# A two-layer hybrid attention block on one Trainium2 core: pooling sums and late forget gates on VectorE, and a planner without its margin

## Chip, core and metric

The kernel runs on one core of a Trainium2 chip, as one program. The metric is the device time of one execution in microseconds; the time of a kernel is the median of several runs.

## What is computed

1024 tokens of width 1024 behind 16 meta tokens (1040 rows) go through two layers. A layer normalizes, projects to 3588 columns, and splits them into three mixers: forgetting attention (4 heads of 64, with a decay `c` summed from forget gates), differential attention (4 heads with two softmaxes each, causal by chunks), and pooling over sliding windows of 2, 4, 8 and 16 rows. Gated outputs go through an output projection and are added to the residual. The reference pads to 1152 rows and cuts again, which the kernel need not do. Cut to what matters here:

```python
for l in range(DEPTH):
    hn = rmsnorm(h, norm_g[l])
    proj = jnp.einsum('bld,de->ble', hn, w_in[l])
    fq, fk, fv, fz, fg, dq, dk, dv, dz, pu, pz = jnp.split(proj, IN_OFFSETS, axis=-1)
    log_f = jax.nn.log_sigmoid(fg.astype(jnp.float32) + b_f[l].astype(jnp.float32))
    c = jnp.transpose(jnp.cumsum(log_f, axis=1), (0, 2, 1))
    a_out = forgetting_attention(...fq, fk, fv, c) * jax.nn.silu(fz)
    b_out = differential_attention(...dq, dk, dv, lam)
    b_out = (rmsnorm(b_out, subln_g[l], SUBLN_EPS) * (1.0 - lambda_init)) * jax.nn.silu(dz)
    c_out = pooling_mixer(pu, w_pool[l], pool_scale[l]) * jax.nn.silu(pz)
    mix = jnp.concatenate([a_out, b_out, c_out], axis=-1)
    h = h + jnp.einsum('ble,ed->bld', mix, w_out[l])
y = rmsnorm(h[:, N_META:N_META + S], final_g)

def pooling_mixer(u, w_pool, pool_scale):
    ...
    pooled = (cs - lower) / cnt[None, :, :, None] - uf
    y = jnp.einsum('blgc,gcd->blgd', pooled.astype(u.dtype), w_pool)
    return y.reshape(B, Lp, POOL_W) * pool_scale
```

## The kernel before

**Precision and projections.** Every float32 product is made of three matmuls of split operands: a rounded high part and the low rest of each side (high x high, high x low, low x high). ScalarE copies the high part, VectorE or GpSimd subtracts to get the low one. The normalized input is held transposed in SBUF as `HT` (high and low part, 8 blocks of 128). A projection item (`proj_chunk`) has 128 output columns in three chunks of some 346 rows; a chunk is 24 matmuls of `HT` and a weight tile `ws` into a PSUM bank `psP`, of which there are two, and an evacuation. So a matmul group can start only when the bank two groups ahead has been read.

**Units.** A layer has six attention units of 128 columns: two of forgetting attention, four of differential. While the projections of a unit run, the attention of the unit before it is slipped in between their matmuls, in steps: scores into `psS` (three banks), softmax on VectorE and ScalarE into `p`, transposes of `p` into `psT` (two banks), a copy and a subtraction into `pp`, and products with the values into `psO` (one bank). A unit of forgetting attention has eight tasks, one of differential attention four: 64 tasks in two layers. The meta tokens' share of a task goes its own way: `thrice` copies 32 columns of `p` three times into `m3`, TensorE transposes 96 columns, and `ptm` gets two high parts and a low one (`meta_t`, `meta_av`).

**Pooling.** Beside the last unit run four more items (`pool_item`, `pool_gate`). `pool_item` writes two halves `Y[1]`, then `Y[0]`; `pooling` makes the window sums of one half by shifted adds between rows `wa` and `wb` (four for `Y[1]`, two for `Y[0]`; on GpSimd), with a copy on ScalarE, and a scaled sum on VectorE back into `Y`. `pool_mix` splits `Y` into `pu` (ScalarE, then VectorE), multiplies with `w_pool` in `mix` (three matmuls in a `psP` bank) and evacuates on VectorE, scaled by `sc`. `pool_gate` then multiplies `Y` by the silu of its gate.

**Output projection.** `out_proj` keeps `w_out` in the place of `HT` and makes eight tiles of 128 rows and one of 16 for the meta rows, 48 matmuls of 512 columns for a full one. VectorE adds the residual into `res`, `rms` normalizes it in place, and beside the last tile of layer 0 `to_hnT` starts to transpose the normalized rows into `HT` for layer 1 (bank `psS`, ScalarE copies, VectorE subtracts).

**Forget gates.** `forget_gates` gives 36 columns to TensorE: three chunks of 16 matmuls with `wg` at the head of a layer, then a copy, an add, and `gate_sums`, which writes the running sums `c` to DRAM, from where the first two units load them as `cb`.

**Order.** Two planners in the kernel set it. `Planner.run` writes the program: after every six matmuls of a projection it takes the attention steps whose inputs a coarse clock (`Clock`) holds ready, with `MARGIN` nanoseconds added. `Order` then lists all instructions with costs of its own and sets each engine's order anew: TensorE's instructions lie in a few lines, each with a fixed order (projections, three queues of steps, deferred ones, transposes for `HT`), and the head that can go first is taken; among heads that can all go at once the one written first. The DMA queue of SyncE is ordered in the same way. Engines run strictly in that order.

```python
heads = [(self.when(q[0]) + MARGIN, q) for q in self.queues if q]
due = [q for t, q in heads if t <= clk.now and (q[0]["target"] <= spent or not live)]
```

## Time and profile before

| what | value |
|---|---|
| median of 3 runs | 1239.56 us (1238.59 to 1240.54) |
| profiled execution | 1240.62 us |
| its span | 1238.8 us |
| TensorE busy | 1199.4 us, 97% (7644 matmuls) |
| VectorE busy | 805.1 us, 65% |
| ScalarE busy | 628.4 us, 51% |
| GpSimd busy | 499.1 us, 40% |

The span runs from the first to the last instruction of the profiled execution; its device time has 1.8 us more around it. Busy time of TensorE says that a matmul was in the pipe, not that it ran at its peak. Layer 0 takes the first 540 us with its last unit from about 470, its output projection goes to about 635, layer 1 to 1140 with its last unit from about 1066, and the rest is the last output projection. PEclk in a row is the clock that TensorE was granted, as a share of 2.4 GHz.

### The profile page before, as it was taken

Reading aid. Unit: us, or ns where it says so; the run is one execution under the profiler, and the core shown is the slowest. Engines: PE = TensorE matmul, PEld = TensorE weight load, DVE = VectorE, ACT = ScalarE, POOL = GpSimd, SP = SyncE. Lnnn points to the kernel's source line nnn. Section 1 sums busy time; section 2 is a strip of 40 time slices with the busy share of each in tenths; the row PEclk is TensorE's granted clock in tenths of the full one; section 3 lists DMA queues with packets and bytes.
Section 4 is the critical chain, followed back from the end, with each engine's and each line's share of the span. In section 5 each row is a group of like instructions: output and inputs, shape, how many; then the busy total and the mean of one; then the engine's idle time right before and its main releaser. Section 6 shows DMA issues by size and latency. Waiting matters only on the chain.

```text
span 1238.8 us, 21122 instructions
## 1 busy us (share of the span) xinstructions
PE 1199.4 (97%) x7644; PEld 1136.7 (92%) x7644; DVE 805.1 (65%) x2203; ACT 628.4 (51%) x1454; POOL 499.1 (40%) x584
## 2 busy tenths in 40 slices
PE   5999999999999999899999999999999999979997
PEld 4999999999999999878889999999999999979786
DVE  6566767786768777753245568688778686776422
ACT  6455556655555554443235556565556555445322
POOL 4334324335261546254314353242443535343432
PEclk9999999999999999899999999999999999989999
DMA  7121110113222242373111211111232332324431
GB/s 241 27 70 35 52 52 19 34 40 45 55 31 57 50 100 53 100 223 108 47 52 29 59 35 61 44 26 44 40 56 36 44 67 69 60 67 125 141 107 51
DMA packets 101736, 82.12 MB, mean 66 GB/s; under 512 B 19272, under 2 KB 91208, under 8 KB 101632
## 3 DMA queue, kind: packets, MB, share of 16 engines
q1 hardware_dynamic: 101488, 80.52, 26.2%
q8 instruction: 60, 0.98, 0.3%
q14 instruction: 44, 0.36, 0.1%
q10 hardware_dynamic: 144, 0.26, 0.1%
HBM read 66.92 MB, written 13.80 MB: 65 GB/s over the span
## 4 chain that ended last, share of the span: by engine, by line
PE 85%; DVE 7%; ACT 3%; DMA 2%; issue 2%; SPq 0%; POOL 0%; POOLq 0%; ACTq 0%; DVEq 0%
PE psP L511 56%; PE psS L511 14%; PE psO L511 7%; PE psT L517 7%; DVE p L148 3%; DMA wo<-in_w_out_dram 1%; ACT p L148 1%; PE psS L517 1%; DVE pp L148 1%; DMA x<-in_x_dram 1%; PE psT L511 1%; DVE HT L148 0%; SPq L148 0%; DMA m<-in_m_dram 0%; DVE Y L148 0%
## 5 line engine op out<-in xcount | busy, mean ns | idle before, releaser
L511 PE MATMUL psP<-HT,ws 128*128 128x346 f32 (+5 forms) x4032 | 709.0, 325 | 6.6 <-DVE Y L148 6.6
L511 PEld LDWEIGHTS psP<-HT,ws 128*128 128x128 f32 x4032 | 642.5, 190 | 8.1 <-DVE Y L148 7.0
L148 POOL TENSOR_TENSOR ws<-wr,ws 128x512 fp32r<-128x512 f32 x112 | 150.9, 1349 | 223.6 <-ACT ws L148 140.9
L148 POOL TENSOR_TENSOR q<-rq,q 64x256 fp32r<-64x256 f32 (+1 forms) x192 | 147.4, 768 | 158.2 <-DVE q L148 144.9
L148 ACT ACTIVATE p<-p,mx 128x144 f32<-128x144 f32 (+3 forms) x192 | 150.9, 786 | 78.9 <-DVE mx L148 76.2
L511 PE MATMUL psS<-K,q 128*128 128x392 f32 (+9 forms) x696 | 144.5, 326 | 0.5 <-DVE mx L148 0.2
L511 PE MATMUL psO<-pp,VV 128*128 128x256 f32 (+1 forms) x800 | 123.4, 283 | 1.5 <-DVE pp L148 1.1
L148 DVE TENSOR_TENSOR pp<-psT,pp 128x512 fp32r<-128x512 f32 (+1 forms) x160 | 98.4, 634 | 37.2 <-ACT pp L148 35.2
L511 PE MATMUL psP<-HT,ms 128*128 128x512 f32 (+1 forms) x504 | 115.7, 385 | 0.4 <-DVE res L148 0.2
L511 PEld LDWEIGHTS psO<-pp,VV 128*128 128x128 f32 x800 | 110.1, 189 | 3.6 <-DVE pp L148 2.4
L511 PEld LDWEIGHTS psP<-HT,ms 128*128 128x128 f32 x504 | 90.4, 188 | 21.7 <-DVE HT L148 1.9
L511 PEld LDWEIGHTS psS<-K,q 128*128 128x128 f32 (+1 forms) x696 | 106.6, 186 | 3.8 <-DVE mx L148 1.8
L148 ACT ACTIVATE pp<-psT 128x512 fp32r<-128x512 f32 (+1 forms) x160 | 84.3, 551 | 48.0 <-PE psT L517 44.7
L148 ACT ACTIVATE ws<-wr 128x512 fp32r<-128x512 f32 x112 | 70.0, 628 | 44.5 <-issue 18.1
L517 PE MATMUL psT<-identf,p 128*128 128x128 f32 x576 | 88.3, 273 | 4.3 <-DVE p L148 4.1
L517 PEld LDWEIGHTS psT<-identf,p 128*128 128x128 f32 x576 | 68.3, 140 | 8.3 <-DVE p L148 7.2
L511 PE MATMUL psS<-HT,ms 128*128 128x512 f32 (+2 forms) x320 | 75.4, 394 | 0.0
L148 DVE TENSOR_SCALAR p<-p,rd 128x144 f32<-128x144 f32 (+7 forms) x128 | 74.0, 582 | 1.7
L511 PEld LDWEIGHTS psS<-HT,ms 128*128 128x128 f32 (+2 forms) x320 | 57.5, 180 | 16.7
L148 DVE CUSTOM_DVE_ANT_0 p<-psS,dist 128x272 f32<-128x272 f32 (+7 forms) x128 | 61.9, 490 | 12.8 <-PE psS L511 7.0
L148 POOL TENSOR_TENSOR ms<-mr,ms 128x128 fp32r<-128x128 f32 (+2 forms) x39 | 33.1, 856 | 77.1 <-ACT ms L148 74.0
L148 ACT ACTIVATE K<-psP 64x346 fp32r<-64x346 f32 (+1 forms) x72 | 32.6, 453 | 55.0 <-DVE K L148 32.4
(132 smaller groups left out, 1429.5 us busy)
## 6 DMA issues: line engine op xcount, KB each, us to landing
wr<-in_w_in_dram SPq DMA_DIRECT2D x112, 256.0 KB, 2.9
wo<-in_w_out_dram SPq DMA_DIRECT2D x14, 512.0 KB, 3.9
mr<-mix_d SPq DMA_DIRECT2D x14, 320.0 KB, 5.7
cb<-c_d SPq DMA_DIRECT2D x8, 520.0 KB, 4.6
x<-in_x_dram SPq DMA_DIRECT2D x8, 512.0 KB
res<-in_x_dram SPq DMA_DIRECT2D x8, 512.0 KB, 3.9
h_d<-res SPq DMA_DIRECT2D x8, 512.0 KB
res<-h_d SPq DMA_DIRECT2D x8, 512.0 KB, 5.3
```

What stands on the lines that cost most here:

```text
L148: r = f(*args, **kw)
L511: r = nc.tensor.matmul(o, w, m, start=start, stop=stop)
L517: r = nc.tensor.transpose(o, src, ident)
```

## The change

- `pooling`: the shifted adds and the small copies beside them go from GpSimd to VectorE. `split`: the subtraction for `pu` goes from VectorE to GpSimd. `mix`: the evacuation goes from VectorE to ScalarE, with `sc` halved beforehand by a new VectorE instruction.
- Layer 1's forget gates are no longer matmuls. `next_gates` loads the four gate columns of `w_in`, given to the kernel as rows (`wg`), each spread over 128 partitions (four DMAs of 512 KB, in tiles that the q of a unit uses); behind the `rms` of each output projection tile of layer 0 `gate_rows` makes four row sums of products on VectorE. At the head of layer 1 nine transposes and ScalarE copies with the bias bring them to four rows, and `gate_sums` is as before. Layer 0 keeps its matmuls.
- `meta_t`: the tripled copy goes; 32 columns of `p` are transposed, and ScalarE copies the result twice. `thrice` is left for the values alone, with one buffer.
- `MARGIN` goes from 1400 to 0. In `Order`, a write of a `VM` tile counts as one of all of it.

```diff
-MARGIN = 1400
+MARGIN = 0
...
+                if self.place.get(name, ("",))[0] == "VM":
+                    p0, p1, at = 0, 128, [(0, 1 << 20)]
...
+    def next_gates(l):
+
+        bf = small.tile([4, 1], F32, tag="bf", name=nm("bf"), bufs=2)
+        sync.dma_start(bf, b_f[l].rearrange("(f o) -> f o", o=1))
+        gx = row("gx")[:4]
+        gw = [sb.tile([128, D], F32, tag="q", name=nm("gw"), bufs=4) for _ in range(4)]
+        for f in range(4):
+            sync.dma_start(gw[f], c_wg[l, f].partition_broadcast(128))
+
+        gt = small.tile([128, 9, 4], F32, tag="gt", name=nm("gt"), bufs=1)
+        done = []
+
+        def rows(hn, np_, col):
+            g = gt[:np_, len(done)]
+            for f in range(4):
+                junk = sb.tile([128, D], BF16, tag="junk", name=nm("junk"), bufs=1)[:np_]
+                dve.scalar_tensor_tensor(
+                    out=junk, in0=hn, scalar=1.0, in1=gw[f][:np_], op0=ALU.mult, op1=ALU.mult, accum_out=g[:, f : f + 1])
+            done.append((g, np_, col))
+
+        def end():
+            with ordr.line(4):
+                for g, np_, col in done:
+                    pt = psT()[:4, :np_]
+                    transpose(pt, g, identf[:np_, :np_])
+                    act.activation(gx[:, col : col + np_], pt, AF.Identity, bias=bf)
+            gate_sums(l, gx)
+
+        return rows, end
...
-            pt = psT()[:96, :nq]
+            pt = psT()[:32, :nq]
             if b:
-                transpose(pt[:, 0:16], thrice(P[-1], 16), identf[:16, :16])
+                transpose(pt[:, 0:16], P[-1][:, 0:32], identf[:16, :16])
             for i in range(2):
-                transpose(pt[:, b + 128 * i : b + 128 * i + 128], thrice(P[2 * jp + i], 128), identf)
+                transpose(pt[:, b + 128 * i : b + 128 * i + 128], P[2 * jp + i][:, 0:32], identf)
             ptm = keep["m"] = small.tile([96, 272], F32R, tag="ptm", name=nm("ptm"), bufs=2)[:, :nq]
-            act.activation(ptm, pt, AF.Copy)
-            dve.tensor_tensor(out=ptm[32:64], in0=pt[32:64], in1=f32(ptm[32:64]), op=ALU.subtract)
+            act.activation(ptm[0:32], pt, AF.Copy)
+            dve.tensor_tensor(out=ptm[32:64], in0=pt, in1=f32(ptm[0:32]), op=ALU.subtract)
+            act.activation(ptm[64:96], pt, AF.Copy)
...
-            pool.tensor_copy(dst[r, 0:sh], src[r, 0:sh])
-            pool.tensor_tensor(out=dst[r, sh:], in0=src[r, sh:], in1=src[r, : T - sh], op=ALU.add)
+            dve.tensor_copy(dst[r, 0:sh], src[r, 0:sh])
+            dve.tensor_tensor(out=dst[r, sh:], in0=src[r, sh:], in1=src[r, : T - sh], op=ALU.add)
...
             sc = keep["sc"] = sm("sc")
             sync.dma_start(sc, pool_scale[l, 128 * t : 128 * t + 128].rearrange("(p o) -> p o", o=1))
+            dve.tensor_scalar(out=sc, in0=sc, scalar1=0.5, scalar2=None, op0=ALU.mult)
 
         def split(c0, n):
             pp = keep["pp"] = sb.tile([128, 2, 512], F32R, tag="pp", name=nm("pu"), bufs=3)[:, :, :n]
             act.activation(pp[:, 0], ut[:, c0 : c0 + n], AF.Copy)
-            dve.tensor_tensor(out=pp[:, 1], in0=ut[:, c0 : c0 + n], in1=f32(pp[:, 0]), op=ALU.subtract)
+            pool.tensor_tensor(out=pp[:, 1], in0=ut[:, c0 : c0 + n], in1=f32(pp[:, 0]), op=ALU.subtract)
...
-            dve.tensor_scalar(
-                out=ut[:, c0 : c0 + n], in0=pt, scalar1=keep["sc"], scalar2=0.5, op0=ALU.mult, op1=ALU.mult)
+            act.activation(ut[:, c0 : c0 + n], pt, AF.Copy, scale=keep["sc"])
...
+            if l + 1 < DEPTH and n == 0:
+                gate_rows, hns.end = next_gates(l + 1)
...
                 hns.append((res, np_, col))
+                gate_rows(res, np_, col)
...
-        fg_chunk, fg_end = fg or forget_gates(l, HT)
+        fg_chunk, fg_end = fg or (lambda c0, n: None, hns.end)
```

Three places where the order of instructions differs, first the last unit of layer 0. VectorE before (Y_6049 is the second half, Y_6050 the first, whose mix products psP_6510 and psP_6542 are evacuated in the last two rows):

```order
L148 TENSOR_TENSOR ptm_6623<-psT_6616,ptm_6623 32x256
L148 TENSOR_TENSOR pu_6547<-Y_6050,pu_6547 128x346
L148 SCALAR_TENSOR_TENSOR Y_6049<-wb_6470,invw,Y_6049 128x1024
L148 TENSOR_TENSOR hd_6474<-wb_6470,rcnt 128x16
L148 TENSOR_SCALAR p_6336<-p_6336,rd_6348 128x912
L148 TENSOR_TENSOR hd_6474<-hd_6474,Y_6049 128x16
L148 TENSOR_TENSOR n_1439_6379<-rd_6377,nlam_651 128x1
L148 COPY Y_6049<-hd_6474 128x16
L148 RECIPROCAL rd_6417<-den_6415 128x1
L148 TENSOR_SCALAR Y_6050<-psP_6510,sc_6440 128x348
L148 TENSOR_SCALAR Y_6050<-psP_6542,sc_6440 128x346
```

The evacuations now stand on ScalarE, which reads (Y_5966 is the first half, psP_6408 and psP_6440 its mix products, wb_6367 the copy for the second half):

```order
L151 ACTIVATE pu_6413<-Y_5966 128x346
L151 ACTIVATE p_6304,den_6318<-p_6304,mx_6305 128x1040
L151 ACTIVATE pp_6421<-psT_6416 128x512
L151 ACTIVATE th_6436<-psP_6386 128x348
L151 ACTIVATE Y_5966<-psP_6408,sc_6343 128x348
L151 ACTIVATE pu_6445<-Y_5966 128x346
L151 ACTIVATE Y_5966<-psP_6440,sc_6343 128x346
L151 ACTIVATE pp_6477<-psT_6473 128x384
L151 ACTIVATE wb_6367<-wa_6364 64x1040
L151 ACTIVATE Y_5966<-psP_6468,sc_6343 128x346
```

They have left VectorE's order, where they stood behind the second half's scaled sum, for ScalarE's, where they stand behind copies and a gate's tanh and ahead of the second half's wb.

Second, VectorE at the end of layer 0's output projection. Before (res_7494 and res_7571 are the last two row tiles, HT rows are subtractions that feed layer 1):

```order
L148 TENSOR_TENSOR res_7494<-psS_7496,res_7494 128x512
L148 TENSOR_TENSOR res_7494<-psS_7497,res_7494 128x512
L148 SCALAR_TENSOR_TENSOR res_7494<-res_7494,rs_7556,g_6933 128x1024
L148 TENSOR_TENSOR res_7571<-psP_7573,res_7571 128x512
L148 TENSOR_TENSOR HT<-psS_7608,HT 128x4x128
L148 TENSOR_TENSOR HT<-psS_7615,HT 128x4x128
L148 TENSOR_TENSOR HT<-psS_7628,HT 128x8x16
L148 TENSOR_TENSOR HT<-psS_7645,HT 128x4x128
L148 TENSOR_TENSOR HT<-psS_7652,HT 128x4x128
L148 TENSOR_TENSOR res_7571<-psP_7574,res_7571 128x512
L148 TENSOR_TENSOR HT<-psS_7665,HT 128x4x128
L148 TENSOR_TENSOR HT<-psS_7672,HT 128x4x128
```

Now (junk rows are the row sums; res_7452 and res_7537 are the last two row tiles):

```order
L151 SCALAR_TENSOR_TENSOR res_7452<-res_7452,rs_7514,g_6823 128x1024
L151 TENSOR_TENSOR res_7537<-psP_7539,res_7537 128x512
L151 SCALAR_TENSOR_TENSOR junk_7434,gt_6837<-res_7367,gw_6830 128x1024
L151 TENSOR_TENSOR HT<-psS_7574,HT 128x4x128
L151 TENSOR_TENSOR HT<-psS_7581,HT 128x4x128
L151 SCALAR_TENSOR_TENSOR junk_7436,gt_6837<-res_7367,gw_6831 128x1024
L151 TENSOR_TENSOR HT<-psS_7594,HT 128x8x16
L151 SCALAR_TENSOR_TENSOR junk_7438,gt_6837<-res_7367,gw_6832 128x1024
L151 TENSOR_TENSOR HT<-psS_7611,HT 128x4x128
L151 TENSOR_TENSOR HT<-psS_7618,HT 128x4x128
L151 TENSOR_TENSOR res_7537<-psP_7540,res_7537 128x512
L151 SCALAR_TENSOR_TENSOR junk_7517,gt_6837<-res_7452,gw_6829 128x1024
```

Row sums of earlier tiles have come between the subtractions; seven more follow below this piece.

Third, TensorE in layer 1, in the attention of the last unit but one. Before (psT_12933 holds transposes from which ScalarE and VectorE make pp_12938):

```order
L517 MATMUL psT_12933<-identf,p_12662 128x128
L517 MATMUL psT_12933<-identf,p_12751 128x128
L517 MATMUL psT_12941<-identf,p_12662 128x128
L517 MATMUL psT_12941<-identf,p_12751 128x128
L517 MATMUL psT_12941<-identf,p_12662 128x128
L517 MATMUL psT_12941<-identf,p_12751 128x128
L511 MATMUL psP_12920<-HT,ws_12652 128x348 x6
L511 MATMUL psP_12965<-HT,ws_12647 128x346 x6
L511 MATMUL psT_12972<-s_2776_12856,onesr 128x256 x2
L511 MATMUL psO_12981<-pp_12938,VV_11460 128x256 x6
```

Now (psT_12723 and pp_12728 are the same pair):

```order
L523 MATMUL psT_12723<-identf,p_12516 128x128
L523 MATMUL psT_12731<-identf,p_12441 128x128
L523 MATMUL psT_12731<-identf,p_12516 128x128
L523 MATMUL psT_12731<-identf,p_12441 128x128
L523 MATMUL psT_12731<-identf,p_12516 128x128
L517 MATMUL psP_12787<-HT,ws_12554 128x348 x3
L517 MATMUL psO_12803<-pp_12728,VV_11329 128x256
```

Between the last transpose into that bank and the first product with its pp stood four transposes and fourteen other matmuls, and now stand four transposes and three.

## Rows read from the trace of the kernel before

**Rows 1.** The page's first part: TensorE's and VectorE's busy time, share, instructions.
```profile
PE 1199.4 (97%) x7644; PEld 1136.7 (92%) x7644; DVE 805.1 (65%) x2203; ACT 628.4 (51%) x1454; POOL 499.1 (40%) x584
```

**Rows 2.** TensorE's waits: instruction <- releaser: us in total, times, longest.
```profile
...
PE psP L511 <- DVE Y L148: 6.6, 2, 3.6
PE psT L517 <- DVE p L148: 4.1, 7, 0.8
...
PE psP L511 <- ACT pu L148: 2.9, 1, 2.9
...
PE psO L511 <- DVE ptm L148: 1.1, 3, 0.6
PE psO L511 <- DVE pp L148: 1.1, 4, 0.3
```

**Rows 3.** Stretches of both last units: length, engines' busy time, granted clock, DMA.
```profile
504.00:510.00 6.00, 5.48 (x19) 5.49 (x20) 4.79 (x10) 0.69 (x2) 0.93 (x1) 0.50 0.61 215
...
1100.00:1106.00 6.00, 5.72 (x30) 5.33 (x28) 3.21 (x5) 1.70 (x4) 1.73 (x2) 0.72 0.33 93
...
1112.00:1118.00 6.00, 5.73 (x20) 5.73 (x21) 3.79 (x9) 1.37 (x3) 0.89 (x1) 0.50 0.30 96
```

**Rows 4.** Layer 0, timeline from 498: start, us, engine, instruction, idle before.
```profile
501.52 1.28 DVE L148 SCALAR_TENSOR_TENSOR Y<-wb,invw,Y 128x1024 f32<-128x1024 f32 x1
...
503.88 1.07 DVE L148 TENSOR_SCALAR Y<-psP,sc 128x348 f32<-128x348 f32 x2
...
504.52 0.94 PE L511 MATMUL psP<-HT,ws 128*128 128x346 f32 x2 [3.02 <-DVE Y L148]
```

**Rows 5.** Layer 1, timelines from 1076 of GpSimd and of TensorE.
```profile
1078.73 2.12 POOL L148 TENSOR_TENSOR wa<-Y 128x1039 f32<-128x1039 f32 x1 [1.08 <-ACT Y L148]
...
1099.35 0.43 PE L511 MATMUL psP<-pu,wps 128*128 128x348 f32 x1 [2.87 <-ACT pu L148]
...
1112.27 3.83 PE L511 MATMUL psP<-HT,ws 128*128 128x346 f32 x12 [3.57 <-DVE Y L148]
```

**Rows 6.** TensorE's timeline where layer 1 begins.
```profile
633.52 1.47 PE L517 MATMUL psS<-identf,res 128*128 128x128 f32 x12
635.54 1.25 PE L517 MATMUL psS<-identf,res 128*128 128x128 f32 x8 [0.54 <-DVE HT L148]
...
638.23 2.77 PE L511 MATMUL psP<-HT,wg 128*36 128x348 f32 x16
640.84 4.53 PE L511 MATMUL psP<-HT,ws 128*128 128x400 f32 x24
```

**Rows 7.** Layer 0's output projection: a stretch, two instructions, an accumulator's reading.
```profile
560.00:630.00 70.00, 70.00 (x312) 56.60 (x311) 22.75 (x25) 19.48 (x49) 27.99 (x46) 1.00 0.25 79
...
572.33 1.28 DVE L148 SCALAR_TENSOR_TENSOR res<-res,rs,g 128x1024 f32<-128x1024 f32 x1 [2.73 <-ACT ms L148]
572.42 1.52 POOL L148 TENSOR_TENSOR ms<-mr,ms 128x128 fp32r<-128x128 f32 x1 [0.72 <-ACT ms L148]
...
553.98 0.08 DVE L148 DVE_READ_ACCUMULATOR lv<-lv 128x1 f32 x1
```

**Rows 8.** Layer 1, timeline from 1033: the pair of the third place.
```profile
1033.60 1.09 ACT L148 ACTIVATE pp<-psT 128x512 fp32r<-128x512 f32 x2 [2.23 <-PE psT L517]
...
1034.23 1.29 DVE L148 TENSOR_TENSOR pp<-psT,pp 128x512 fp32r<-128x512 f32 x2 [0.91 <-ACT pp L148]
...
1036.00 0.28 PE L511 MATMUL psO<-pp,VV 128*128 128x256 f32 x1
```

**Rows 9.** Instructions of tile m: ns min/median/max, first and last start.
```profile
L148 DVE COPY m<-p x128: 228/248/256, 75.6 to 1128.4; 128x96 f32<-128x96 f32 x128
```

**Rows 10.** DMA issues: count, KB each, median us from issue to landing.
```profile
rs<-v SPq DMA_DIRECT2D x28, 1.0 KB, 1.9
r_d<-rs SPq DMA_DIRECT2D x28, 1.0 KB, 3.2
...
sc<-in_pool_scale_dram SPq DMA_DIRECT2D x4, 0.5 KB, 2.7
```

More of the change, by code (lines that the diff above doesn't have):

```diff
@@ L48, in _width_chunks @@
     return [(c, min(step, w - c)) for c in range(0, w, step)]
+class Rows(list):
+    pass
 class Clock:
@@ L443, in hymba @@
     c_m96,
+    c_wg,
     out,
@@ L589, in thrice @@
     def thrice(src, np_):
-        t = small.tile([128, 96], F32, tag="m3", name=nm("m3"), bufs=3)[:np_]
+        t = small.tile([128, 96], F32, tag="m3", name=nm("m3"), bufs=1)[:np_]
         dve.tensor_copy(t.rearrange("p (r c) -> p r c", r=3), src[:, 0:32].unsqueeze(1).to_broadcast([np_, 3, 32]))
@@ L1503, in hymba @@
                 e["target"] = 0.0
-        hns = []
+        hns = Rows()
         op = out_proj(l, HT, st["sz"], Y, raw, hns)
@@ L1541 @@
     arrays, args = {}, []
-    for name, a in [(n, inputs[n]) for n in _INS] + list(_tables().items()):
+    for name, a in [(n, inputs[n]) for n in _INS] + list(_tables().items()) + [
+        ("wg", inputs["w_in"][:, :, FG : FG + 4].transpose(0, 2, 1))]:
         a = _np.ascontiguousarray(a)
```

## The prediction

> **What bounds the kernel now.** I read the page first. TensorE has 1199.4 of 1238.8 us [rows 1], so the time is TensorE's instruction stream: a change pays only if it takes matmuls out of that stream, takes a wait out of it, or keeps its clock up. The list of TensorE's waits comes next [rows 2]. Beside the first load, which the change does not touch, it holds 6.6 us in two waits for the tile Y, 2.9 us for one wait for pu, and a scatter of short waits in the attention units (4.1 + 1.1 + 1.1 us for p, ptm and pp). Third, the windows show the granted clock: it is 1.00 (2.4 GHz) everywhere but in the first load, at the very end, and in two stretches that follow those Y and pu waits [rows 3], where it is 0.50 (1.2 GHz). So the last unit of each layer, in which the pooling runs, is the one place that loses time in a lump.
>
> **Pooling stage, what it loses now.** In layer 0 VectorE reaches the evacuation of the first mix product only after the scaled sum that waits for the whole window chain; TensorE stands 3.02 us for the bank [rows 4]. Then it works 5.48 us in the stretch 504 to 510 at 0.50 [rows 3], half of which (2.7) is lost. Sum 5.7. In layer 1 the window sums run on GpSimd from 1078.73 on (2.12 us for a full one, with other work between), the first mix product waits 2.87 for pu, and the next projection waits 3.57 for the same evacuation [rows 5]; 0.28 of each of 6 us is lost at 1100 to 1106 (1.7) and half of 5.73 at 1112 to 1118 (2.9) [rows 3]. Sum 11.0. Together 16.7 us.
>
> **What the change puts there.** A window add becomes a VectorE tensor_tensor. The nearest row is the two-input 128x1024 operation of 1.28 us [rows 4, 7] against 2.12 on GpSimd [rows 5]: four adds in the long chain fall from about 8.5 to 5.1 us. The mix evacuations (0.53 each, two in 1.07 [rows 4]) go to ScalarE, so they no longer stand behind the scaled sum of the other tile; the order on ScalarE has one copy of pp and one tanh ahead of the first of them, and the copy for the other chain (wb) only behind two. The subtractions of pu go to GpSimd, which is then free of the windows. Over both layers VectorE gives 12 evacuations and 12 subtractions of about 0.5 (12 us) and takes 12 adds of 1.28 (15 us): nearly even. I expect the Y and pu waits to shrink to under 1.5 us in a layer, too short for the clock to fall: **-14**. Bounds: all of it, -16.7; half of it, -8, if new short waits in the crowded VectorE order take their place.
>
> **Forget gates.** Three groups of 16 matmuls leave the head of layer 1; the first holds TensorE from 638.23 to 640.84 [rows 6], 2.6 us: -7.7 for three, a little under 3 x 2.6 since the other two have two columns fewer. Nine transposes come; 12 of 128 columns take 1.47 [rows 6], 0.12 each, so +1.0. Net **-6.7**, one answer. On VectorE 36 row sums come, 1.28 each as the like operation on 128x1024, and 0.08 to read the accumulator [rows 7]: 49 us. In the 70 us from 560 to 630 VectorE is busy 22.75 and TensorE never waits [rows 7]; it runs 312 matmuls there, 6.5 tiles of 48 at 10.8 us, so the sums add 6.5 x 4 x 1.36 = 35, together 58 of 70. They fit, but the order leaves 13 of them among the last transposes, where VectorE's subtractions feed HT and TensorE already waits (0.54 in [rows 6], the longest of three). Walking that order with these durations, four row sums stand ahead of the subtractions that the first projection needs, and TensorE waits about 2.5 instead of 0.5: **+2**. Bounds -1 (the sums are done early) and +8 (VectorE comes 4 us late there and the clock falls once, at 2 to 3 us as above).
>
> What a row shows of the port: a GpSimd subtraction of 128x128 took 1.52 us at 572.42, beside a VectorE operation of 1.28 that began 0.09 earlier [rows 7]; GpSimd stood still until VectorE was done. The Trainium skill ("SBUF — State Buffer", Who interferes with whom) says the same as a rule: a VectorE instruction with two SBUF inputs and a GpSimd instruction that reads SBUF block each other whole. The rule speaks against the row sums: by it GpSimd's 28.0 us [rows 7] do not overlap the 35 us of sums, and the sum of this part would be by it +7 in place of +2.
>
> **MARGIN 1400 to 0.** This moves every attention step. A step used to be placed when the planner's clock was 1.4 us past the time at which it thought the data ready; now at once. So TensorE has less other work between two steps. An example is drawn in the order above, in layer 1's last but one unit: ScalarE takes up the transposed tile at 1033.60, VectorE has the first low part at about 1034.9 (two in 1.29 from 1034.23), TensorE asks for it at 1036.00, 1.1 us later [rows 8]. Now only four transposes (0.11 each) and three projection matmuls (0.16 each, as the 16 of 2.6 us in [rows 6]) stand between: TensorE asks 0.9 us after the transposes' end, 0.4 too early. Over all 160 such pairs the TensorE work between, counted in the order at these durations, falls from a median of 3.6 us to 2.75, and in the lowest tenth from 2.75 to 1.5; the chain needs 1.1 to 1.5 us where its engines are free. For p, the pairs stay above the shortest chain. So most steps stay covered and some 30 of the 160 do not. The price has no row: it is bounded below by 0 (a wait once taken gives the steps behind it time), and above by about 20 us (each of those 30 and as many of ptm and p waiting 0.3). Nearest are the short waits of today, 4.1 + 1.1 + 1.1 = 6.3 us [rows 2], that 1.4 us of slack left over; I take a doubling, **+7**. I exclude a gain: no wait of today is shortened by earlier asking.
>
> **The rest: 0.** The tripled copies (136 of 0.25 us, 128 of them in [rows 9]) leave VectorE, and ScalarE copies ptm twice; ScalarE is at half load, and TensorE's transposes keep their number. If VectorE were full in the units this would be worth up to the 6.3 us of short waits; I leave it inside +7. The row sums' weights are 2.1 MB more on SP's queue, issued among the loads of w_out; they hide behind the last units, and would cost what w_out then comes late. The halving of sc on VectorE now waits for a DMA that stands on SP's queue behind rs, r_d and vr; see rival two.
>
> **Sum.** -14 - 6.7 + 2 + 7 = -11.7. The profiled execution took 1240.62 us (1.8 around the span): 1228.9. It lies 1.1 above the median of the runs shown, so the forecast for the median is **1228**.
>
> **Rivals.** One, slower: the short waits grow instead of doubling. The place is the psO matmuls of the attention units, the price 0.12 us for each of 224 chains (160 pp, 64 ptm) = 27 us instead of 7: 1248. For it: the example above loses 0.4 in one step. Against it: one wait covers the chains behind it, and VectorE loses 34 us of copies. It decides from about 0.085 us a chain, 19 us, where the gains of 18.7 are gone. Chance 0.17.
>
> Two, the wait moves: VectorE's halving of sc stands in its order ahead of gate products and pp subtractions, and every mix evacuation needs it. Its DMA comes behind v, rs (1.9 to land), the power, r_d (3.2) and vr on SP's queue, and takes 2.7 itself [rows 10]: with about 3 us of issuing and of ScalarE and GpSimd work, 11 us from the sums matmul, while TensorE's own work up to the need, counted in the order, is 13 to 14. If it comes 3 us late in both layers and the clock falls again, 10 of the 14 are lost: 1238. The change then does not do in the pooling stage what it says. Chance 0.13.
>
> Three, the row sums crowd VectorE and GpSimd as the port row has it: +8 to +9 at the end of the output projection, 1235, still faster. For it the 1.52 us subtraction, against it the whole tile time (10.8 us) that each result has. Chance 0.10.
>
> **Chances and range.** Forecast 0.60 (1215 to 1236 by its bounds), the rivals 0.17, 0.13, 0.10. A measurement of this kernel tells 0.2%, 2.5 us, from no change. Faster by over 0.2% are the forecast and rival three, 0.70; within it rival two, 0.13; slower rival one, 0.17. The range reaches from the low bounds (-16.7 - 6.7 - 1 = -24.4, 1215) up to 1243, which takes in rivals two and three and leaves out most of rival one.
>
> **What would show it.** In the profile after: no Y wait over 1.5 us and the clock at 1.00 through both last units (the -14); no wg matmuls in the second head, and waits for HT there of 2 to 3 us (the -4.7); psO and psT waits for pp, ptm and p of 10 to 17 us in all instead of 6.3 (the +7). The forecast is wrong if these exceed 25, or if the clock falls again near sc or HT.

## The result, and the profile after

The changed kernel takes 1226.35 us (median of 4 runs, 1224.48 to 1226.85) against 1240.05 for the kernel before beside it: ratio 0.9887, interval 0.9870 to 0.9904. The forecast was 1228, range 1215 to 1243. The profiled execution spans 1222.7 us, 16.1 less than before.

The page's first part, which answers [rows 1]: TensorE has 10.7 us less work, VectorE 8.9 more, and still two thirds of the span.

```profile
PE 1188.7 (97%) x7605; PEld 1120.7 (92%) x7605; DVE 814.0 (67%) x2137; ACT 658.3 (54%) x1536; POOL 493.5 (40%) x572
```

The list of TensorE's waits (instruction <- releaser: us in total, times, longest), which answers [rows 2]:

```profile
PE psT L523 <- DVE p L151: 3.0, 5, 1.8
...
PE psP L517 <- DVE K L151: 2.0, 1, 2.0
PE psS L523 <- DVE HT L151: 1.9, 3, 1.0
PE psP L517 <- DVE th L151: 1.5, 1, 1.5
PE psP L517 <- ACT Y L151: 1.5, 2, 1.2
```

The 6.6 us for Y and 2.9 for pu have become 1.5 for Y, 1.5 for a gate's th and a little for pu. The waits of the attention units have not grown: p stands at 3.0 (1.8 of it in one wait of layer 1's last unit), and pp and ptm have nearly gone. A wait of 2.0 us for K is new; nothing in the forecast stands for it.

The windows of the two last units answer [rows 3] (columns as there):

```profile
498.00:504.00 6.00, 6.00 (x41) 5.93 (x41) 4.02 (x10) 3.08 (x7) 1.69 (x2) 1.00 0.01 3
504.00:510.00 6.00, 5.65 (x37) 5.17 (x35) 3.12 (x11) 3.53 (x9) 4.37 (x4) 1.00 0.97 349
...
1100.00:1106.00 6.00, 6.00 (x40) 6.00 (x38) 5.48 (x13) 3.44 (x7) 3.89 (x4) 1.00 0.44 160
1106.00:1112.00 6.00, 4.00 (x26) 3.48 (x25) 5.18 (x8) 2.53 (x6) 3.73 (x4) 1.00 0.75 264
```

In the timelines (start, us, engine, instruction, idle before), which answer [rows 4, 5], a window add takes 1.23 us on VectorE (eleven of the twelve do; one, at 492.92 beside a GpSimd subtraction, takes 2.35), where GpSimd took 2.12, and the waits of TensorE beside the pooling are these, two of layer 0 and two of layer 1:

```profile
1093.41 1.23 DVE L151 TENSOR_TENSOR wa<-Y 128x1039 f32<-128x1039 f32 x1
```

```profile
497.73 0.75 PE L517 MATMUL psP<-pu,wps 128*128 128x346 f32 x3 [1.21 <-ACT Y L151]
...
511.18 1.86 PE L517 MATMUL psP<-HT,ws 128*128 128x348 f32 x10 [1.53 <-DVE th L151]
...
1097.29 2.17 PE L517 MATMUL psP<-HT,ws 128*128 128x346 f32 x12 [0.29 <-ACT Y L151]
...
1108.55 0.55 PE L523 MATMUL psT<-identf,p 128*128 128x128 f32 x3 [1.83 <-DVE p L151]
```

The granted clock is 1.00 (2.4 GHz) in all four windows, though TensorE works only 4.00 of 6 us in the last of them. That is the one stretch of layer 1's last unit that still loses much; before, two long waits and two stretches below full clock stood there [rows 3, 5].

**Where the time went.** Waits alone don't give the sum, so I used one measure for all kernels: the time from one projection matmul to another (the same two of the 4032 in every kernel), less the time that the matmuls between them would take at the median spacing of their kind and shape in the kernel before. What is left over is lost. Each line is one profiled execution; a second one of the changed kernel (after_again, below) differs from the first by 0.3 or less in three columns, and by about 1 us in the head of layer 1 and in the last column. The levels hang on how a spacing is counted, so read the differences between kernels.

| us lost | layer 0, attention (matmuls 96 to 1824) | last unit and output projection (to 2016) | head of layer 1 (to 2304) | attention (to 3744) | last unit to the end |
|---|---|---|---|---|---|
| before | 5.3 | 11.0 | 0.0 | 0.7 | 13.4 |
| after | 5.1 | 5.2 | 3.6 | 3.6 | 3.6 |

The two columns with a last unit give 15.6. The matmuls themselves give 6.6 more. The head of layer 1 takes 3.6 back and the attention units 2.7. That is 15.9, close to the 16.1 by which the span became shorter.

### The profile page after: what moved, and what is told of

It reads as the page before. It is cut to its first block, busy times and chain, and to the rows that moved or that the text cites. A ratio compares the mean times of both kernels' runs of the same rounds, so it can differ in the third digit from the quotient of the medians.

```text
span 1222.7 us, 21035 instructions
## 1 busy us (share of the span) xinstructions
PE 1188.7 (97%) x7605; PEld 1120.7 (92%) x7605; DVE 814.0 (67%) x2137; ACT 658.3 (54%) x1536; POOL 493.5 (40%) x572
## 4 chain that ended last, share of the span: by engine, by line
PE 86%; DVE 5%; ACT 3%; DMA 2%; issue 2%; SPq 1%; POOL 1%; POOLq 0%; ACTq 0%; DVEq 0%
PE psP L517 55%; PE psS L517 15%; PE psO L517 8%; PE psT L523 7%; DVE p L151 1%; SPq L151 1%; DMA r_d<-rs 1%; PE psS L523 1%; PE psT L517 1%; ACT K L151 1%; DVE K L151 1%; DMA sc<-in_pool_scale_dram 1%; ACT ptm L151 0%; DMA x<-in_x_dram 0%; DVE ptm L151 0%
## 5 line engine op out<-in xcount | busy, mean ns | idle before, releaser
L517 PE MATMUL psP<-HT,ws 128*128 128x346 f32 (+5 forms) x4032 | 730.3, 325 | 3.9 <-DVE K L151 2.0
L517 PE MATMUL psO<-pp,VV 128*128 128x256 f32 (+1 forms) x800 | 129.2, 283 | 0.2
L523 PE MATMUL psT<-identf,p 128*128 128x128 f32 (+1 forms) x704 | 114.5, 273 | 3.3 <-DVE p L151 3.0
L517 PEld LDWEIGHTS psO<-pp,VV 128*128 128x128 f32 x800 | 113.1, 189 | 2.0 <-DVE pp L151 0.9
L523 PEld LDWEIGHTS psT<-identf,p 128*128 128x128 f32 (+1 forms) x704 | 81.3, 132 | 10.8 <-DVE p L151 4.7
L151 ACT ACTIVATE ptm<-psT 32x256 fp32r<-32x256 f32 (+1 forms) x128 | 47.5, 371 | 63.1 <-DVE ptm L151 45.0
L517 PEld LDWEIGHTS psS<-HT,ms 128*128 128x128 f32 (+2 forms) x320 | 57.5, 180 | 16.7
L151 DVE TENSOR_TENSOR K<-psP,K 64x346 fp32r<-64x346 f32 (+1 forms) x72 | 37.2, 517 | 47.4 <-ACT K L151 46.8
L151 POOL TENSOR_TENSOR ms<-mr,ms 128x128 fp32r<-128x128 f32 (+2 forms) x39 | 39.1, 1010 | 68.7 <-ACT ms L151 68.6
```

Source lines behind the costliest of these rows:

```text
L151: r = f(*args, **kw)
L517: r = nc.tensor.matmul(o, w, m, start=start, stop=stop)
L523: r = nc.tensor.transpose(o, src, ident)
```

## Experiments

Each kernel was timed beside the kernel before on the same chip; ratios are to that one. "Changed kernel" is the one forecast.

### One part put back: t_back, p_back, g_back, m_back

If the terms of the forecast add up, putting a part back costs what the part was worth.

```diff
t_back:
-MARGIN = 0
+MARGIN = 1400
p_back (window, pu's subtraction, mix evacuation; no halving of sc):
-            dve.tensor_tensor(out=dst[r, sh:], in0=src[r, sh:], in1=src[r, : T - sh], op=ALU.add)
+            pool.tensor_tensor(out=dst[r, sh:], in0=src[r, sh:], in1=src[r, : T - sh], op=ALU.add)
...
g_back (next_gates and gate_rows are not called):
-        fg_chunk, fg_end = fg or (lambda c0, n: None, hns.end)
+        fg_chunk, fg_end = fg or forget_gates(l, HT)
m_back (meta_t as before, m3 with three buffers):
-                transpose(pt[:, b + 128 * i : b + 128 * i + 128], P[2 * jp + i][:, 0:32], identf)
+                transpose(pt[:, b + 128 * i : b + 128 * i + 128], thrice(P[2 * jp + i], 128), identf)
```

> The changed kernel with MARGIN put back to 1400, nothing else. The forecast's term of +7 for MARGIN 0 says about 1219 (1226.35 less 7), with short waits of the attention units back near 6 us. A rival read from the two traces says that the term is small: layer 0's attention loses the same before and after, and of the 6 us that layer 1's attention gives back 2.0 are one wait for K behind the gates' running sums; then 1223 to 1226. A second rival: asking earlier also brings the pooling stage's steps forward, and with the margin back the time is above 1228.

> The changed kernel with the pooling part undone (windows on GpSimd, pu's subtraction and the mix evacuation on VectorE, no halving of sc). The forecast's term of 14 says 1240; the whole of what the two last units lost (16.7) says 1243, with the Y and pu waits and the clock of 0.50 back in both. If the waits went by the new order of the margin and not by the engines, the time stays below 1235.

> The changed kernel with layer 1's forget gates as matmuls again, as in layer 0. By the forecast (6.7 saved, 2 lost at the transition) 1231. By the trace after, which shows 2.0 us more in one wait for K behind the gates' running sums, 1229. If the row sums crowd VectorE and GpSimd so that they cost what the matmuls did, 1226 or less.

> The changed kernel with the tripled copies back on VectorE (m3 with three buffers), the only part that the forecast left without a number of its own. If VectorE's 34 us of copies stand in nobody's way, 1226 to 1227; if VectorE is what the short waits of the attention units hang on, up to 6 us more, 1232.

| kernel | median, us | ratio, interval | median less 1226.35 |
|---|---|---|---|
| t_back | 1235.11 | 0.9966 (0.9957 to 0.9975) | +8.8 |
| p_back | 1235.43 | 0.9976 (0.9965 to 0.9987) | +9.1 |
| g_back | 1230.79 | 0.9936 (0.9918 to 0.9953) | +4.4 |
| m_back | 1236.36 | 0.9975 (0.9962 to 0.9989) | +10.0 |

The medians are not all from one stretch of runs; by the ratios, each taken beside the kernel before on its own chip, the four cost 10, 11, 6 and 11 us. By medians they sum to 32 us, where the whole change is worth 13.7. So the parts do not add. Only the gates come out near the forecast (4.7). The margin, which was to cost 7, saves 8.8 here. The copies, which got 0, are worth as much as the pooling part (two of m_back's ten runs took 1230 and 1232, the others 1236 to 1237). For p_back and m_back the times lie outside what was expected. By the measure above, this is where:

| us lost | layer 0, attention | last unit and output projection | head of layer 1 | attention | last unit to the end |
|---|---|---|---|---|---|
| t_back | 1.4 | 11.9 | 4.1 | 1.5 | 11.5 |
| p_back | 5.1 | 10.9 | 3.1 | 3.7 | 9.8 |
| g_back | 5.1 | 8.7 | 0.5 | 3.1 | 4.8 |
| m_back | 6.7 | 10.7 | 3.3 | 1.8 | 10.4 |

t_back has two answers in one row. In the attention units the margin of 1400 does save time: 1.4 and 1.5 instead of 5.1 and 3.6, 5.8 us together. In the last units it loses 14.6. m_back and p_back lose there too. p_back has its waits for Y back, longer than in [rows 2]; g_back's 8.7 is of a profiled run of 1232.30 us, 1.5 above its median.

```profile
PE psP L517 <- DVE Y L151: 7.4, 2, 5.1
```

The longest of p_back's waits is not VectorE's order alone. Before that evacuation, in layer 0, VectorE itself stands 2.13 us for the load of sc, which is taken up below:

```profile
503.64 1.07 DVE L151 TENSOR_SCALAR Y<-psP,sc 128x348 f32<-128x348 f32 x2 [2.13 <-DMA sc<-in_pool_scale_dram]
```

### One part alone: p_alone, t_vm

```diff
p_alone, against the kernel before:
-            pool.tensor_tensor(out=dst[r, sh:], in0=src[r, sh:], in1=src[r, : T - sh], op=ALU.add)
+            dve.tensor_tensor(out=dst[r, sh:], in0=src[r, sh:], in1=src[r, : T - sh], op=ALU.add)
...
+            dve.tensor_scalar(out=sc, in0=sc, scalar1=0.5, scalar2=None, op0=ALU.mult)
...
-            dve.tensor_scalar(
-                out=ut[:, c0 : c0 + n], in0=pt, scalar1=keep["sc"], scalar2=0.5, op0=ALU.mult, op1=ALU.mult)
+            act.activation(ut[:, c0 : c0 + n], pt, AF.Copy, scale=keep["sc"])
t_vm, against the kernel before:
-MARGIN = 1400
+MARGIN = 0
...
+                if self.place.get(name, ("",))[0] == "VM":
+                    p0, p1, at = 0, 128, [(0, 1 << 20)]
```

> The kernel before with the pooling part alone (windows and the halved sc on VectorE, pu's subtraction on GpSimd, the mix evacuation on ScalarE); margin, tripled copies and gates as before. If the parts of the change add up, as the forecast took it, the 14 us come from this part: 1225. If the last units lose their time because VectorE comes late there, and the windows load it further, this part alone gains little or nothing, 1236 to 1242, with waits for VectorE's s, rd or ptm in place of those for Y and pu.

> The kernel before with MARGIN 0 and the whole-tile rule for VM, nothing else. Forecast's term: +7, 1246, from short waits in the attention units. If the margin works mainly in the last units, where steps asked for earlier leave less to do beside the pooling, 1232 to 1238. If the attention units lose some 4 us and the last units stay as they are (their Y and pu waits are set by GpSimd's windows), 1242 to 1244.

p_alone: 1242.29 us, ratio 1.0026 (1.0016 to 1.0036), 3 us slower than before. t_vm: 1238.37, ratio 0.9985 (0.9975 to 0.9996). The pooling part, to which the forecast gave 14 us, gives nothing by itself. In p_alone layer 0's last unit loses 15.0 us (11.0 before) and layer 1's 9.9 (13.4 before). In t_vm the five columns are 5.6, 11.6, 0.6, 1.7 and 7.0: without the pooling part the margin costs 1.3 in the attention units, and layer 1's end gains 6.4. There TensorE's wait for pu falls from 2.9 to 0.4, and VectorE does not stand for sc ahead of the evacuation. So the margin has a gain in that last unit that is not the load of sc, told in the next section; no run shows why.

### Where the last units lose: the load of sc

The reason shows in t_back. Its windows in layer 1's last unit (columns as in [rows 3]):

```profile
1100.00:1106.00 6.00, 1.17 (x7) 0.83 (x6) 5.91 (x16) 3.49 (x7) 0.91 (x2) 0.75 0.48 150
1106.00:1112.00 6.00, 3.62 (x12) 3.35 (x13) 2.79 (x9) 2.68 (x6) 3.68 (x4) 0.50 0.27 95
```

TensorE works 1.17 and 3.62 of 6 us, at a granted clock of 0.75 and then 0.50. Its timeline there (start, us, engine, instruction, idle before):

```profile
1095.39 0.49 PE L517 MATMUL psP<-pu,wps 128*128 128x348 f32 x2
...
1098.27 0.64 PE L517 MATMUL psP<-pu,wps 128*128 128x346 f32 x3
...
1102.33 0.38 PE L517 MATMUL psO<-ptm,VM 96*128 96x256 f32 x1 [1.40 <-ACT ptm L151]
1107.19 0.55 PE L517 MATMUL psT<-s,onesr 128*128 128x256 f32 x1 [4.47 <-DVE s L151]
1108.93 3.83 PE L517 MATMUL psP<-HT,ws 128*128 128x346 f32 x12 [1.19 <-ACT Y L151]
```

The mix products at 1095.39 and 1098.27 fill both psP banks. Until one is read, no projection can start. TensorE has only attention steps left, runs into their chains (ptm, then s, 4.47 us), and gets its next projection at 1108.93, released by ScalarE's evacuation of Y. That evacuation waits for sc; here are ScalarE, then VectorE's halving, then SyncE's queue, in the same stretch:

```profile
1108.33 0.99 ACT L151 ACTIVATE Y<-psP,sc 128x348 f32<-128x348 f32 x2 [0.65 <-DVE sc L151]
```

```profile
1108.14 0.34 DVE L151 TENSOR_SCALAR sc<-sc 128x1 f32<-128x1 f32 x2 [0.43 <-DMA sc<-in_pool_scale_dram]
```

```profile
1095.99 7.68 SPq L151 DMA_DIRECT2D wo<-in_w_out_dram  x3
1103.72 0.90 SPq L151 DMA_DIRECT2D sc<-in_pool_scale_dram  x2
```

And what SyncE's queue waited for from 1095 to 1104 (instruction <- releaser: us in total, times, longest):

```profile
SPq L151 <- DVE wb L151: 5.1, 1, 5.1
...
SPq L151 <- DVE hd L151: 1.5, 1, 1.5
```

Three loads of w_out stand ahead of the two sc loads. Two of them (128x1024) go where the window rows wa and wb were, and so wait until VectorE has read those: 5.1 us until the add into wb, 1.5 until the hd that reads it. sc, half a kilobyte, is issued at 1103.72 and VectorE has it at 1108.14. The windows that now run on VectorE thus hold up, by way of two loads that are needed only in the output projection, the evacuation that had been freed from VectorE. In the changed kernel sc stands ahead of those loads:

```profile
1092.91 0.90 SPq L151 DMA_DIRECT2D sc<-in_pool_scale_dram  x2
1098.65 7.84 SPq L151 DMA_DIRECT2D wo<-in_w_out_dram  x3
```

```profile
1096.68 0.99 ACT L151 ACTIVATE Y<-psP,sc 128x348 f32<-128x348 f32 x2
```

sc is issued at 1092.91 and the evacuation runs at 1096.68. TensorE waits 0.3 for it. In p_alone the queue reads as in t_back, and TensorE's wait for Y is 4.6 us in one piece:

```profile
1102.97 6.17 SPq L148 DMA_DIRECT2D wo<-in_w_out_dram  x3
1109.19 0.90 SPq L148 DMA_DIRECT2D sc<-in_pool_scale_dram  x2
```

```profile
PE psP L511 <- ACT Y L148: 4.6, 1, 4.6
```

The order on SyncE's queue is known for every kernel with the pooling part, so it can be set beside what the last unit of layer 1 loses:

| sc in layer 1 | kernels, us lost from there to the end |
|---|---|
| ahead of the 128x1024 loads of w_out | after 3.6, g_early 3.8, g_back 4.8, t_last0_ge 5.6, t_last0 6.0 |
| behind them | p_alone 9.9, m_back 10.4, m_last_e500 10.8, m_last 11.2, t_back 11.5 |

(The last kernels follow below.) No kernel with sc behind is better than 9.9, none with sc ahead is worse than 6.0. In layer 0 sc stands behind in t_back, p_alone and m_last_e500, which lose 11.3 to 15.0 there. Of the kernels with sc ahead, t_last0, t_last0_ge, m_last and m_back lose more than 10 in layer 0 too, by a second cause told under the hardware. In g_back (8.7) sc is ahead as well, but VectorE still stands 2.61 us for its load, and TensorE waits 2.2 for Y.

How far this is shown: in t_back and p_alone the rows give the whole chain in layer 1, and the load is what ends the wait. In m_last, m_last_e500 and m_back it is not the last to end it (see m_last_e500 below). The table is ten kernels' orders set beside their times, and they differ in more than the place of sc. A kernel that only loads sc earlier was not tried.

### Margin or copies in the last unit only: t_last0, m_last

```diff
t_last0 (MARGIN = 1400):
-                heads = [(self.when(q[0]) + MARGIN, q) for q in self.queues if q]
+                heads = [(self.when(q[0]) + (MARGIN if q[0]["unit"] % 6 < 5 else 0), q) for q in self.queues if q]
m_last (meta_t; the tripled copies as before in this branch, m3 with three buffers):
+            if st["place"] == 5:
+                pt = psT()[:96, :nq]
...
+                return
```

> The changed kernel with MARGIN 0 only for the attention steps of the last unit of each layer, and 1400 for the other five. If the gain of the margin lies in the last unit and its cost in the others, this takes the gain without the cost: 1220 to 1224. If the steps of the units before must be early too, so that the last unit starts with no backlog, it is near the run with 1400 everywhere, 1231 to 1236.

> The changed kernel with the tripled copies back on VectorE in the last unit of each layer alone (some 20 of 136 copies, 5 us of VectorE). If VectorE's load beside the pooling sets the end of the last units, most of the 10 us that all copies cost come back: 1232 to 1236. If the copies cost by their sum over the six units, a sixth of it: 1227 to 1229.

t_last0: 1227.56 us, ratio 0.9900 (0.9865 to 0.9934), with single runs from 1221.67 to 1234.23. m_last: 1238.78, ratio 1.0000 (0.9990 to 1.0011). Both lie outside what was expected, t_last0 between its two ranges and m_last above both. t_last0's profiled run, of 1230.72 us, is one of its slower ones. So the last unit alone decides both. With the margin at 0 only there, nearly all of its gain is back, and the attention units lose 1.7 and 1.5 as in t_back. With 17 copies put back only there, the whole of what the change gained is gone.

### Order or load on VectorE: m_last_e500

In m_last's layer 1 TensorE waited 3.69 us for a pp whose subtraction stood behind the second window add and the scaled sum on VectorE. I took that order for the cause, and moved only those subtractions ahead.

```diff
-                        d = (t, -ops[k]["way"], k, t, e)
+                        d = (t + ops[k]["late"], -ops[k]["way"], k, t, e)
...
+                ordr.late = -500 if st["place"] == 5 else 0
                 split_psum(pp[:, 0, :n], pp[:, 1, :n], pt[:, :n])
+                ordr.late = 0
```

> The run m_last (tripled copies in the last units) with one thing changed: in the planned order VectorE prefers the low parts of pp in the last units by 0.5 us, so that they stand ahead of the second window add and the scaled sum, as they do in the changed kernel. If m_last's loss is the order on VectorE (a pp behind the window chain), the wait of 3.7 us for pp goes and the time is 1227 to 1231. If it is the 5 us of copies as load, it stays at 1237 to 1240.

It measured 1240.05 us, ratio 1.0006 (0.9997 to 1.0014). The theory fell. TensorE's timeline, m_last first, then m_last_e500:

```profile
1107.25 0.79 PE L517 MATMUL psO<-pp,VV 128*128 128x256 f32 x5 [3.69 <-DVE pp L151]
...
1112.63 3.83 PE L517 MATMUL psP<-HT,ws 128*128 128x346 f32 x12 [0.30 <-ACT Y L151]
```

```profile
1108.72 0.58 PE L518 MATMUL psO<-ptm,VM 96*128 96x256 f32 x1 [4.29 <-DVE ptm L151]
...
1113.05 3.83 PE L518 MATMUL psP<-HT,ws 128*128 128x346 f32 x12 [0.30 <-ACT Y L151]
```

The wait for pp is gone, and a wait of 4.29 for ptm stands in its place. In both the projections come back only at 1113, behind the evacuation that waits for the halved sc. The load of sc is issued at 1105.86 in the one and 1106.75 in the other, behind the w_out loads. But here the load is not what ends the wait. VectorE in m_last:

```profile
1111.62 0.16 DVE L151 RECIPROCAL rd<-den 128x1 f32<-128x1 f32 x1 [0.44 <-ACT p L151]
...
1111.85 0.14 DVE L151 TENSOR_SCALAR sc<-sc 128x1 f32<-128x1 f32 x1
```

The halving runs 6.0 us after the issue (4.4 in t_back and 4.2 in p_alone, where VectorE stood for the load), without a wait of its own, behind attention work that had waited for ScalarE's p. In m_last_e500 and m_back it stands in the same way. So VectorE's order holds sc last, for an estimated 1 to 2 us by the difference of these times; that the planner put the halving so late because it counted the load late is likely, but no run shows it. Nor is it the 5 us of copies as load: between 1097 and 1111 VectorE runs none of them in m_last. What the copies changed is the planned order, on SyncE's queue and on VectorE.

### The wait for K: g_early, after_again, t_last0_ge

```diff
g_early:
+        if l:
+            fg_end()
         while todo:
...
-        fg_end()
+        if not l:
+            fg_end()
t_last0_ge: both this and the line of t_last0
```

> The changed kernel once more, as the measure for the runs beside it on the same chip: 1226, as it was.

> The changed kernel with the end of the late gates (nine transposes, running sums) written ahead of layer 1's first projections, so that VectorE's order has the whole chain of running sums ahead of the first K evacuation; the last units keep their order. If the wait of 2.0 us for K comes from VectorE standing at that chain, it is gone: 1224. If the row sums of the last tile, which end only at 651, are what is late, the wait moves to K or HT and the time stays at 1226.

> MARGIN 1400 in five units and 0 in the last (as t_last0) with the gates' end written early (as g_early). If both hold by themselves: 1227.6 less 2 to 3 for the wait for K, 1222 to 1226, below the changed kernel; the spread of t_last0 (1221.7 to 1234.2) says that single runs will scatter.

after_again: 1225.70 us (1224.83 to 1226.70). g_early: 1221.36 (1221.29 to 1223.84), ratio 0.9858 (0.9845 to 0.9872), 4.3 us under after_again and the fastest kernel of the study. t_last0_ge: 1225.43, ratio 0.9882 (0.9867 to 0.9898). VectorE's timeline in the changed kernel, with the wait on TensorE behind it:

```profile
675.10 0.51 DVE L151 TENSOR_TENSOR K<-psP,K 64x346 fp32r<-64x346 f32 x1
675.64 2.31 DVE L151 TENSOR_TENSOR_SCAN mn<-gx,na 4x1040 f32<-4x1040 f32 x1
677.99 0.52 DVE L151 TENSOR_TENSOR K<-psP,K 64x346 fp32r<-64x346 f32 x1
```

```profile
678.65 5.63 PE L517 MATMUL psP<-HT,ws 128*128 128x346 f32 x34 [2.03 <-DVE K L151]
```

A running sum of 2.31 us stands between two K subtractions, and the projection needs the bank that the second one reads. In g_early the same sum is at 660.26 and the first K at 665.63:

```profile
660.26 3.30 DVE L151 TENSOR_TENSOR_SCAN mn<-gx,na 4x1040 f32<-4x1040 f32 x1
...
665.63 0.51 DVE L151 TENSOR_TENSOR K<-psP,K 64x348 fp32r<-64x348 f32 x1
```

No wait for K remains, and the head of layer 1 loses 0.4 instead of 3.6, which is most of the 4.3. Not all of that is K: the wait of 0.95 us for HT where layer 1 begins is gone in g_early too, and the stretch around it loses 0.1 instead of 1.2. after_again has the same wait for K, of 2.06 us, and there the granted clock falls to 0.72 behind it, where it stayed at 1.00 in the first profile:

```profile
678.00:684.00 6.00, 4.87 (x21) 4.90 (x22) 1.46 (x3) 0.98 (x2) 1.50 (x1) 0.72 0.27 64
```

t_last0_ge has no wait for K either, and its attention units lose 1.6 and 1.7, but its layer 0 loses 13.8 in the last unit and output projection. It is 2.1 us faster than t_last0, whose single runs scatter over 12.6, so whether the two edits add stays open.

## Why the prediction was right, and where it was not

The sum was right: -11.7 forecast, -13.7 measured. That it came so near is in part luck, for two of its terms stand on something other than what they name. As terms of the whole change:

- **Pooling stage, -14** (bounds -16.7 to -8): 15.6 less lost in the two columns with a last unit. What was forecast is there: no Y wait over 1.5 us, clock at 1.00 (Y and pu together are 1.6 us in layer 0, a little over the 1.5, with 1.5 for th beside them). The assignment of it does not hold. I gave the term to the engines alone, and p_alone gives nothing. The evacuation left VectorE's queue for ScalarE, but there it needs sc halved, and whether that comes in time was settled by the orders that the margin and the copies gave. Giving each part a price of its own was the step that failed.
- **Rival two, chance 0.13.** It named this very wait, priced at 10 us, and put the halving of sc behind r_d and vr on SyncE's queue. In the changed kernel it shows in small: TensorE waits 1.2 and 0.3 us for Y. In t_back, m_back, p_alone and m_last it came in full, in one layer or both, with the load behind another blocker, the w_out loads (in m_back and m_last the halving then stood on VectorE as well). So the forecast was nearer to its edge than 0.13 says: the likeliest case held because of two edits that I had counted as a cost and as nothing.
- **Forget gates, -6.7:** the matmuls give 6.6. **Transition, +2:** the wait for HT is 0.95 us, against 2.5 forecast (0.54 in [rows 6]), and the stretch around it loses 1.2. What I missed is the last link of the gates' chain. The running sum kept its time (674.84 before, 675.64 after) while TensorE's work behind it came 10 us earlier, and so fell among the K subtractions: 2.0 us in one wait, 2.4 of the head's 3.6. I had followed the row sums to their end and not who reads their result.
- **MARGIN, +7:** 2.7 more lost in the attention units in all, 5.8 against t_back. The size is near in that place, the mechanism is not: the sign that was named, waits for pp, ptm and p of 10 to 17 us, did not come. In the two attention stretches TensorE's waits over 0.15 us are 3.0 us in all, against 5.2 before and 3.8 in t_back. What grew is how often a run of projection matmuls is broken by a step: 418 times there, 281 before, 293 in t_back (418 in t_vm). So the time lies in the spacing of the matmuls and not in waits; that the breaks cost it is read from these counts and was not tested. "I exclude a gain" was wrong: I looked for it only where a step is asked for, and the gain lies in how the last units are ordered.
- **Rival one**, the short waits at 27 us: the list of waits shows none of it: pp, ptm and p are 3.5 us in all. **Rival three**, row sums against GpSimd: in the 70 us from 560 on VectorE is now busy 54 of 70 (forecast 58, [rows 7] had 22.75) and TensorE never waits:

```profile
560.00:630.00 70.00, 70.00 (x321) 56.83 (x321) 54.03 (x77) 18.45 (x45) 34.52 (x40) 1.00 0.20 70
```

- **The rest, 0:** the tripled copies are worth 10 us in the changed kernel, the other large miss. That VectorE leaves 34 us free is not what pays: with only 17 of the 136 copies back, m_last loses as much as m_back and more.

## What to carry to other kernels

Where a planner orders the queues, an edit need not have a price of its own: p_alone lost 3 us and t_vm gained 1, and with either put back the changed kernel loses 9. Cost the whole change as one order, and for every wait that is to vanish look up what the new waiter needs and what stands ahead of that on its queue, down to a half-kilobyte load behind a megabyte. And when work is taken out of TensorE's stream, follow what was hidden behind it: what keeps its clock time falls on whatever moves up.

## What the hardware showed

A GpSimd subtraction can stand for as long as VectorE runs two-input operations on SBUF back to back. In t_last0, at the start of layer 0's output projection, GpSimd and then VectorE:

```profile
530.99 5.65 POOL L151 TENSOR_TENSOR s<-sq,s 128x256 fp32r<-128x256 f32 x1 [0.73 <-DVE s L151]
```

```profile
530.76 3.09 DVE L151 TENSOR_TENSOR HT<-wo,HT 128x512 fp32r<-128x512 f32 x5
533.77 0.48 DVE L151 SCALAR_TENSOR_TENSOR sz<-sz,gs,vr 128x256 f32<-128x256 f32 x1
534.17 1.88 DVE L151 TENSOR_TENSOR HT<-wo,HT 128x512 fp32r<-128x512 f32 x3
```

```profile
PE psT L517 <- POOL s L151: 3.6, 1, 3.6
```

The same subtraction of s took 0.73 us elsewhere (at 513.45 in the changed kernel). Here it took 5.65 and ended at 536.64, after VectorE's eight subtractions of w_out and the product between them (to 536.05), and TensorE waited 3.6 for it, with the granted clock at 0.72 from 536 to 542. m_last, m_back and t_last0_ge have that wait too, of 3.8 to 4.0 us. It is the second cause in layer 0 named above. The Trainium skill ("SBUF — State Buffer", Who interferes with whom) says that a VectorE instruction with two SBUF inputs contends with a GpSimd instruction that reads SBUF; the trace agrees, and shows one GpSimd instruction held across several of VectorE. In the changed kernel GpSimd's s comes at 530.80 and takes 1.12; from 531.23 to 531.99 VectorE runs there a product with one input in PSUM and a cast, which have one SBUF input each. GpSimd is not always held so long. Among the row sums of the changed kernel, where each sum is followed by a short accumulator read, the two engines take turns (GpSimd's subtraction, then VectorE's sums before and behind it):

```profile
571.70 2.21 POOL L151 TENSOR_TENSOR ms<-mr,ms 128x512 fp32r<-128x512 f32 x1 [1.69 <-ACT ms L151]
```

```profile
571.54 1.20 DVE L151 SCALAR_TENSOR_TENSOR junk<-res,gw 16x1024 bf16<-16x1024 f32 x1
...
572.79 2.19 DVE L151 SCALAR_TENSOR_TENSOR junk<-res,gw 16x1024 bf16<-16x1024 f32 x1
```

GpSimd ends at 573.91, some 1.2 after the first sum does, and the second sum, which takes 1.2 undisturbed, ends at 574.98. Why GpSimd gets in here and not between the subtractions of w_out was not tested.
